# The ends of two mixers in a written order: rows stored as normed, scale and shift behind the gather, three blocks routed during the fourth, lists ahead of weights

## The chip, the cores and the metric

The kernel runs on one core of one Trainium2 chip. The metric is device time in microseconds of one execution, lower is better. A core has five engines with instruction queues of their own: TensorE (PE, matrix products and transposes), VectorE (DVE), ScalarE (ACT), GpSimd (POOL) and SyncE (SP), which here only issues transfers. ScalarE and GpSimd issue transfers too. Products are written to PSUM, everything else lies in SBUF, and inputs and weights come from HBM.

## What is computed

Two transformer blocks in a row on 512 tokens of width 1024, in float32. Each has a mixer and a mixture of experts. In the first, the experts are chosen in two levels (one of four groups, then two of its four experts); in the second, four of 32. Cut to what the change touches:

```python
# block 1, after the mixer
x = layer_norm(ALPHA * x + (1 + gt_m) * mix, ln1_g, ln1_b)
u = layer_norm(x) * (1 + sc_f) + sh_f        # no gain of its own: scale and shift by column
ffn = hierarchical_moe(u, ...)               # 16 experts, silu(u @ gate) * (u @ up) @ down
# block 2, after the mixer
x = x + gt1 * rmsnorm(y, g_post_mix)
h2 = rmsnorm(x, g_pre_ffn) * (1 + sc2) + sh2
f = moe_ffn(h2, w_router, b_router, w_gu, b_gu, w_dn, b_dn)   # 32 experts, top 4 of softmax
```

## The kernel before

Four stages follow one another: mixer1, moe1, mixer2, moe2. Tokens lie in four blocks (`c` = 0 to 3) of 128 rows. Matrix products are made in three passes on values split into a high part (`whi`, `xh`, written by ScalarE) and a low part (`wlo`, `xl`, written by VectorE as the difference).

**The end of a mixer.** mixer1 makes block `c` of its output with `tail_mm`, normalises it (`tail_norm`), stores it (X1), takes the statistics of the second norm, transposes the rows (`tail_turn`) for the router's logits, and `tail_u` writes the rows that the experts will read: ScalarE applies the norm, GpSimd multiplies by the row `1 + sc_f` and adds the row `sh_f` (L696, L697), and the result goes to HBM (U1). mixer2 does the same with `out_mm`, `tail_norm`, `tail_turn` and `tail_u`; there GpSimd multiplies by one row (L2188) and VectorE finishes (L2205) before the rows go to U2. The Tile scheduler orders all this by readiness and priority.

**Routing and lists.** When the logits of all four blocks are there, `route1` (or its twin at the end of mixer2) takes the top values, makes softmax weights, and `weights_of` makes a one-hot for each choice, the `mask` of chosen experts and their weights `comb`. `lists` turns the mask into each token's position in its expert's list by products with triangular ones (`pos`), and splits `comb` into three bfloat16 pieces (`w3`) in `aux`, beside the token's number. For an expert, `list_hot` marks which token stands at which place, `list_sum` multiplies that with `aux`, and `list_end` reads out the rows to gather (`ig`), to scatter (`isc`) and their weights (`slw`).

**The experts.** moe1 and moe2 run in an order written out by hand: steps (one for each weight slice), with hooks at step numbers. Up to 52 blocks of 128, 96, 64 or 32 rows are gathered from U by an indirect transfer on GpSimd's queue (`x_gather`), transposed on TensorE into PSUM (`x_turn`, tile `pt`), and split there into `xh` and `xl` (`x_split`); blocks of few rows stay whole and are copied (L1015). Weights come in 1 MB loads, most of them on SyncE's queue, into `wraw`, and are split by ScalarE and VectorE slice by slice. The first loads of a stage stand behind its first gather on GpSimd's queue. `plan` orders the experts' remainders into blocks once the counts are known; it runs on GpSimd (L854 on) in six pieces at the steps of the table PLAN, and gives SyncE the expert numbers (`exi`) for its further loads. mixer2's weight of the output and moe1's last loads share SyncE's queue with this.

## Time and profile before

| | us |
|---|---|
| median of three runs | 2361.54 |
| range of the runs | 2360.82 to 2361.91 |
| profiled execution | 2365.56 |
| its span | 2363.7 |

| stage | TensorE busy | VectorE busy | transfers busy |
|---|---|---|---|
| 420 to 700 us (moe1) | 247.48 of 280 | 179.50 of 280 | 0.94 |
| 1300 to 2364 us (moe2) | 955.53 of 1064 | 571.97 of 1064 | 0.98 |

A window row gives, for a stretch, the busy time of each engine in us, the granted clock of TensorE as a share of full, and the share of the sixteen transfer engines. A timeline row gives the start and the length of an instruction, what it writes and reads, and in brackets how long its engine stood idle before it and what ended that. Stages are limited by different things, so each row is read in its own stage.

### The profile page before, as it was taken

What the parts mean: (1) busy time and instruction counts of PE and PEld (TensorE: products, weight loads), DVE (VectorE), ACT (ScalarE), POOL (GpSimd) and SP (SyncE); (2) the same over time, 40 slices, a digit from 0 to 9 for tenths busy, and PEclk for the clock granted to TensorE, in tenths of its full rate; (3) what the DMA queues carried; (4) which work ended last, traced back from release to release, by engine and by line L of the source; (5) the groups of instructions that cost most, each with busy time, mean ns of one, the idle gap of its engine ahead of it and who ended that gap; (6) DMA issues with size and microseconds to landing.
All of it is one profiled execution on the core that took longest, in us unless ns stands there. A gap on an engine that the chain in (4) does not pass through costs nothing. (4 is left out here: it accounts for less than half of the span.)

```text
span 2363.7 us, 31489 instructions
## 1 busy us (share of the span) xinstructions
PE 2118.9 (90%) x11221; PEld 1357.3 (57%) x11221; DVE 1385.6 (59%) x2687; ACT 1024.0 (43%) x1560; POOL 432.8 (18%) x405
## 2 busy tenths in 40 slices
PE   6999996779997999999987989979999997999993
PEld 2656664446665887778865445635555563554551
DVE  5555597645786856664466456545455553654663
ACT  3332454435674544553234444424344433443553
POOL 2001223311312120000024211312211031112100
PEclk9999896989998999999997999989999998999996
DMA  9766446998986423313357999999999989999996
GB/s 291 241 205 237 177 172 257 353 355 309 356 292 205 103 76 111 109 58 118 130 181 282 383 405 399 363 375 403 403 395 395 405 342 379 403 401 398 398 409 229
DMA packets 174659, 679.80 MB, mean 288 GB/s; under 512 B 21293, under 2 KB 61061, under 8 KB 116129
## 3 DMA queue, kind: packets, MB, share of 16 engines
q1 hardware_dynamic: 151632, 606.83, 67.5%
q0 software_dynamic: 22576, 69.85, 10.6%
q8 instruction: 90, 1.47, 0.3%
q10 hardware_dynamic: 288, 1.05, 0.1%
q14 instruction: 73, 0.59, 0.1%
HBM read 642.29 MB, written 35.46 MB: 287 GB/s over the span
## 5 line engine op out<-in xcount | busy, mean ns | idle before, releaser
L121 DVE TENSOR_TENSOR wlo<-wraw,whi 128x1024 fp32r<-128x1024 f32 (+1 forms) x535 | 646.3, 1232 | 333.7 <-ACT whi L120 324.6
L120 ACT ACTIVATE whi<-wraw 128x1024 fp32r<-128x1024 f32 (+1 forms) x535 | 552.6, 1055 | 344.5 <-PE pm L83 124.7
L83 PE MATMUL pm<-whi,xh 128*96 128x512 f32 (+1 forms) x704 | 283.9, 404 | 15.1 <-ACT whi L120 15.0
L83 PE MATMUL pm<-wlo,xh 128*96 128x512 f32 (+1 forms) x704 | 281.0, 402 | 6.1 <-DVE wlo L121 5.5
L83 PE MATMUL pm<-wraw,xh 128*32 128x512 f32 (+1 forms) x1344 | 238.3, 617 | 12.6 <-DMA wraw<-in_w_gu 12.6
L83 PE MATMUL pm<-whi,xl 128*96 128x512 f32 (+1 forms) x608 | 243.0, 400 | 0.0
L996 POOL DMA_INDIRECT xg<-U,ig x52 | 88.5, 1701 | 631.2 <-issue 275.8
L1240 POOL DMA_INDIRECT Y<-eo,isc x52 | 99.2, 1908 | 402.8 <-ACT eo L1239 103.2
L83 PEld LDWEIGHTS pm<-whi,xh 128*96 128x96 f32 (+1 forms) x704 | 125.3, 178 | 64.3 <-ACT whi L120 20.4
L83 PEld LDWEIGHTS pm<-wraw,xh 128*32 128x32 f32 (+1 forms) x1344 | 68.1, 126 | 151.3 <-issue 124.0
L83 PEld LDWEIGHTS pm<-wlo,xh 128*96 128x96 f32 (+1 forms) x704 | 119.6, 170 | 50.3 <-DVE wlo L121 8.8
L83 PE MATMUL po<-wlo,ah 128*96 128x512 f32 (+1 forms) x304 | 124.2, 409 | 12.7 <-DVE wlo L121 12.4
L83 PE MATMUL po<-wraw,ah 128*32 128x512 f32 (+1 forms) x672 | 132.6, 620 | 1.9 <-DMA wraw<-in_w_dn 1.9
L83 PE MATMUL po<-whi,ah 128*96 128x512 f32 (+1 forms) x304 | 126.8, 417 | 8.1 <-ACT whi L120 6.3
L83 PEld LDWEIGHTS pm<-whi,xl 128*96 128x96 f32 (+1 forms) x608 | 106.4, 175 | 36.8
L83 PE MATMUL po<-whi,al 128*96 128x512 f32 (+1 forms) x304 | 121.8, 401 | 0.8 <-DVE al L1204 0.8
L1008 PEld LDWEIGHTS pt<-ident,xg 64*128 64x128 f32 (+3 forms) x416 | 56.5, 199 | 100.8 <-issue 51.8
L1008 PE MATMUL pt<-ident,xg 64*128 64x64 f32 (+3 forms) x416 | 70.0, 294 | 47.8 <-DMA xg<-U,ig 47.1
L1017 ACT ACTIVATE xh<-pt 128x384 fp32r<-128x384 f32 (+2 forms) x56 | 28.2, 504 | 130.1 <-PE pt L1008 114.8
L83 PE MATMUL px<-hh,whi 128*128 128x512 f32 x192 | 77.3, 403 | 0.6 <-DVE gsum L766 0.6
L83 PE MATMUL px<-hh,wlo 128*128 128x512 f32 x192 | 76.6, 399 | 0.0
L83 PE MATMUL px<-hl,whi 128*128 128x512 f32 x192 | 76.6, 399 | 0.0
(630 smaller groups left out, 3774.1 us busy)
## 6 DMA issues: line engine op xcount, KB each, us to landing
wraw<-in_w_gu SPq DMA_DIRECT2D x254, 1024.0 KB
wraw<-in_w_dn SPq DMA_DIRECT2D x126, 1024.0 KB
wraw<-in_w_e_down SPq DMA_DIRECT2D x31, 1024.0 KB
wraw<-in_w_e_gate SPq DMA_DIRECT2D x30, 1024.0 KB
wraw<-in_w_e_up SPq DMA_DIRECT2D x30, 1024.0 KB
wraw<-in_w_in SPq DMA_DIRECT2D x58, 512.0 KB
mz<-in_w_ada SPq DMA_DIRECT2D x80, 256.0 KB
wraw<-in_w_mod SPq DMA_DIRECT2D x26, 512.0 KB
```

The lines of the kernel that those rows point to most:

```text
L83: self.nc.tensor.matmul(out, lhsT, rhs, start=start, stop=stop)
L120: nc.scalar.activation(h, v, AF.Copy)
L121: nc.vector.tensor_sub(l, v, h.bitcast(F32))
L996: self.nc.gpsimd.indirect_dma_start(out=B.xg[0:B.n, :], out_offset=None, in_=self.U, in_offset=bass.IndirectOffsetOnAxis(ap=B.ig[:, :1], a ...
L1008: self.nc.tensor.transpose(B.xt[:, k * n:k * n + n], B.xg[0:n, 4 * h2 + k:1024:8], self.ident[0:n, 0:n])
L1017: nc.scalar.activation(B.xh[:, d, 0:n], pv, AF.Copy)
L1240: nc.gpsimd.indirect_dma_start(out=self.Y[:, :], out_offset=bass.IndirectOffsetOnAxis(ap=B.isc[:, :1], axis=0), in_=o, in_offset=None, com ...
```

## The change

It rewrites the end of both mixers and moves one step of arithmetic behind the gather.

- U1 and U2 hold the rows as normed: one pass of ScalarE with scale (and bias). GpSimd's row operations, VectorE's last pass in mixer2 and the broadcast rows are gone. The stores of blocks 2 and 3 are issued by ScalarE's queue in mixer1, by SyncE's in mixer2; the store of block 3's X1 goes to GpSimd's queue.
- `x_split` applies scale and shift to the transposed rows, where they are numbers per partition: four VectorE operations per half of a gathered block, in PSUM (or, for whole blocks, straight into the copy).
- The order from the last output product of mixer1, and from the second half of mixer2's products, is written by hand on TensorE, VectorE, ScalarE and GpSimd. Blocks 0 to 2 are routed up to the mask while block 3's root is worked out (`together` takes one operation of each in turn); block 3 follows alone.
- The mask is written as bfloat16. `lists` is divided: positions, the first experts' indices from three columns of `aux`, and only then softmax weights, `comb` and its three pieces.
- `rsqrt` loses one operation and writes to its target; in mixer2 two roots can run as one of width 2.
- `plan` runs on VectorE up to `exi`, at earlier steps. `ehalf` is made once at the start.
- Dummy products of the identity with itself (`warm`) are put into TensorE's order: 9 and 4 in mixer1, 8 and 4 in mixer2.

The core of the diff:

```diff
-PLAN = {2: (-4, -3, -1, 0, 1, 2), 1: (-4, -3, -1, 0, 1, 2)}
+PLAN = {2: (-11, -10, -9, -8, 1, 2), 1: (-11, -10, -9, -8, 1, 2)}
...
+    def together(self, *gs):
+        gs, r = list(gs), [None] * len(gs)
+        left = list(range(len(gs)))
+        while left:
+            for i in list(left):
+                try:
+                    next(gs[i])
...
         def tail_u(c):
-            cs = slice(c * 128, c * 128 + 128)
-            yc = y[:, c, :]
             u = wk.tile([128, 1024], F32, name="u", tag="L")
-            nc.scalar.activation(u, yc, AF.Identity, scale=sts[c][:, 1:2], bias=sts[c][:, 2:3])
-            nc.gpsimd.tensor_mul(u, u, rows[2])
-            nc.gpsimd.tensor_add(u, u, rows[3])
-            (nc.sync if c == 3 else nc.gpsimd).dma_start(self.U1[cs, :], u)
+            nc.scalar.activation(u, y[:, c, :], AF.Identity, scale=sts[c][:, 1:2], bias=sts[c][:, 2:3])
+            (nc.scalar if c > 1 else nc.gpsimd).dma_start(self.U1[c * 128:c * 128 + 128, :], u)
...
+            root = tail_stats(3)
+            l3 = tail_logits(3)
+            self.logit_end(R, 2, l2, sts[2][:, 1:2], sts[2][:, 0:1])
+            self.together(root, self.route1_steps(R.lg, Q, 0, 3))
+            self.logit_end(R, 3, l3, sts[3][:, 1:2], sts[3][:, 0:1])
+            tail_bias(3)
+            self.warm(9)
+            self.run_mod(self.route1_steps(R.lg, Q, 3, 1))
+            tail_u(3)
+            self.lists_pos()
+            self.warm(4)
+            ohs = self.lists_first(FIXED[1], lambda b: self.half_tile(wk.tile([128, 512], F32, name="loh", tag="P", bufs=7)))
+            self.route1_end(R.lg, Q, sm)
+            self.lists_comb(ohs)
...
+    def warm(self, n):
+        ps = self.pt.tile([128, 512], F32, name="pt")
+        for _ in range(n):
+            self.mm(ps[:, 0:128], self.ident, self.ident, True, True)
...
     def plan(self, fixed, pairs):
         nc, sm, L = self.nc, self.esm, self.L
-        ve, E = nc.gpsimd, L.E
+        ve, E = nc.vector, L.E
...
+        if self.xcols:
+            g, s = self.xcols
+            f = lo if B.col else pv
+            for k in range(4):
+                j = 4 * h2 + k
+                nc.vector.tensor_scalar(f[:, k, :], pv[:, k, :], g[:, j:j + 1], s[:, j:j + 1], op0=OP.mult, op1=OP.add)
+            pv = f
...
         def tail_u(c):
             q = xr[c // 2][:, c % 2, :]
-            nc.vector.scalar_tensor_tensor(q, q, rr[:, c:c + 1], rows[2], op0=OP.mult, op1=OP.add)
-            nc.gpsimd.dma_start(self.U2[c * 128:c * 128 + 128, :], q)
+            nc.scalar.activation(q, y[:, c, :], AF.Copy, scale=nr[:, c + 1, 1:2])
+            (nc.sync if c > 1 else nc.gpsimd).dma_start(self.U2[c * 128:c * 128 + 128, :], q)
...
+            for c in range(2):
+                out_end(c, 1, out_mm(c, 1, W))
+            tail_sum(0)
+            self.run_mod(root(0))
+            tail_norm(0)
+            out_end(2, 1, out_mm(2, 1, W))
+            tail_sum(1)
+            self.run_mod(root(1))
+            tail_norm(1)
+            tail_turn(0)
+            ps = out_mm(3, 1, W, None, range(4))
+            l0 = tail_logits(0)
+            tail_turn(1)
...
+            out_end(3, 1, out_mm(3, 1, W, ps, range(4, 8)))
```

VectorE at the end of mixer1, from the mask to the first indices, before (`ohk` one-hot of the choices, `ew` weights, `slsb` the sum read out):

```order
L807 TENSOR_REDUCE mask<-ohk 128x64
L1528 RECIPROCAL s_3359<-s_3359 128x4
L817 CAST maskb<-mask 128x64
L1529 TENSOR_TENSOR ew<-s_3359,gw 128x4
L1530 TENSOR_TENSOR ew<-ew,e_3358 128x4
L808 TENSOR_TENSOR ohk<-ohk,ew 128x128
L827 SCALAR_TENSOR_TENSOR pos<-px,mask 128x64
L809 TENSOR_REDUCE comb<-ohk 128x64
L829 TENSOR_SCALAR pos<-pos 128x64
L840 COPY cnt<-px 128x16
L921 CAST aux<-comb 128x64
L929 TENSOR_TENSOR oh<-slots,pos 128x512
```

and with the change:

```order
L896 TENSOR_REDUCE maskb<-ohk 128x16
L933 SCALAR_TENSOR_TENSOR pos<-px,maskb 128x64
L935 TENSOR_SCALAR pos<-pos 128x64
L1049 TENSOR_TENSOR loh<-slots,pos 128x512 x2
L1067 COPY slsb_3398<-pt 128x3
L972 TENSOR_SCALAR plank<-cnt 128x16
L1071 TENSOR_TENSOR slf_3402<-slsb_3398 128x1
L973 TENSOR_TENSOR plank<-plank,slots 128x16
L1072 CAST ig_3400<-slf_3402 128x1
```

The weights and their split are no longer between positions and indices, and the first pieces of the plan (`plank`) stand there instead.

VectorE at the start of moe1, from the end of the lists to the first block's split, before:

```order
L954 TENSOR_REDUCE slw<-slsb 128x1
L858 TENSOR_REDUCE planc<-plano 16x1
L1019 TENSOR_TENSOR xl<-pt,xh 128x512
L861 TENSOR_REDUCE planc<-plano 16x1
L1019 TENSOR_TENSOR xl<-pt,xh 128x512
L121 TENSOR_TENSOR wlo<-wraw,whi 128x1024 x4
```

and with the change:

```order
L1042 CAST aux<-w3r_3432 128x64
L1043 TENSOR_TENSOR aux<-w3r_3432,aux 128x64
L957 TENSOR_REDUCE slw_3442<-pt 128x1
L957 TENSOR_REDUCE slw_3449<-pt 128x1
L996 CAST exi<-plan 1x16
L1152 TENSOR_SCALAR pt<-pt,g_1894,s_1896 128x128 x4
L1159 TENSOR_TENSOR xl<-pt,xh 128x512
L1152 TENSOR_SCALAR pt<-pt,g_1894,s_1896 128x128 x4
L1159 TENSOR_TENSOR xl<-pt,xh 128x512
L121 TENSOR_TENSOR wlo<-wraw,whi 128x1024 x4
```

Weights' pieces, their sums and `exi` now stand here, and the four operations of scale and shift ahead of each half's low part.

ScalarE at the end of mixer2 (`q` squares: of a product `px` with `ss`, of normed rows `y`; `uT` and `rows` transposes copied out, `l` logits), before:

```order
L2178 ACTIVATE q_11526,ss_4299<-px 128x512
L2192 ACTIVATE q_11548,ss_4299<-y_11301 128x1024
L2178 ACTIVATE q_11591,ss_4299<-px 128x512
L2192 ACTIVATE q_11613,ss_4299<-y_11301 128x1024
L2178 ACTIVATE q_11656,ss_4299<-px 128x512
L2192 ACTIVATE q_11678,ss_4299<-y_11301 128x1024
L2199 ACTIVATE uT<-pt 128x512 x2
L778 ACTIVATE l_11755<-px 128x128
L2199 ACTIVATE rows_11302<-pt 128x512 x2
```

and with the change:

```order
L2341 ACTIVATE q_11673,ss_4351<-px 128x512
L2362 ACTIVATE q_11693,nv<-y_11431 128x1024
L2341 ACTIVATE q_11720,ss_4351<-px 128x512
L2362 ACTIVATE q_11743,nv<-y_11431 128x1024
L2370 ACTIVATE uT<-pt 128x512 x2
L858 ACTIVATE l_11780<-pw 128x128
L2370 ACTIVATE rows_11432<-pt 128x512 x2
L2362 ACTIVATE q_11815,nv<-y_11431 128x1024
L2383 ACTIVATE xr_11434<-y_11431,nr 128x1024
L2341 ACTIVATE q_11832,ss_4351<-px 128x512
L858 ACTIVATE l_11844<-pw 128x128
L2370 ACTIVATE uT<-pt 128x512 x2
```

The copies of block 0's and 1's transposes now stand ahead of the square of block 3's product, behind the squares of the normed rows of blocks 0 and 1.

## Rows read from the trace of the kernel before

**Rows 1.** Windows by stage: PE, PEld, DVE, ACT, POOL busy; clock; DMA share; GB/s
```profile
370.00:380.00 10.00, 0.90 (x22) 0.82 (x22) 6.31 (x36) 0.20 (x1) 3.15 (x5) 0.50 0.26 89
1240.00:1250.00 10.00, 0.81 (x18) 0.72 (x18) 9.64 (x31) 0.00 (x0) 3.31 (x4) 0.50 0.01 2
420.00:700.00 280.00, 247.48 (x1229) 160.11 (x1229) 179.50 (x305) 157.08 (x227) 61.91 (x45) 0.93 0.94 342
1300.00:2364.00 1064.00, 955.53 (x4682) 528.85 (x4674) 571.97 (x801) 443.36 (x553) 193.72 (x139) 0.95 0.98 382
```

**Rows 2.** Timeline of GpSimd, end of mixer1: start, length, instruction, idle before
```profile
353.55 2.86 POOL L697 TENSOR_TENSOR u<-u,rows 128x1024 f32<-128x1024 f32 x1
...
376.55 1.05 POOL L996 DMA_INDIRECT xg<-U,ig  x1 [7.80 <-DVE slf L949]
```

**Rows 3.** Timeline of GpSimd, end of mixer2
```profile
1247.75 1.60 POOL L996 DMA_INDIRECT xg<-U,ig  x1 [0.18 <-issue]
```

**Rows 4.** Timeline of VectorE, end of mixer1
```profile
354.70 1.73 DVE L155 SCALAR_TENSOR_TENSOR rs<-rs,rs 128x1 f32<-128x1 f32 x1
...
357.78 1.28 DVE L674 SCALAR_TENSOR_TENSOR ymix<-ymix,rs,rows 128x1024 f32<-128x1024 f32 x1
...
371.38 0.20 DVE L817 CAST maskb<-mask 128x64 bf16<-128x64 f32 x1
...
375.54 0.15 DVE L950 CAST ig<-slf 128x1 int32<-128x1 f32 x1
```

**Rows 5.** Timeline of VectorE, end of mixer2
```profile
1229.98 3.44 DVE L2205 SCALAR_TENSOR_TENSOR xr<-xr,rr,rows 128x1024 f32<-128x1024 f32 x1
...
1238.03 0.25 DVE L785 SCALAR_TENSOR_TENSOR lg<-px,rr,br 128x32 f32<-128x32 f32 x1 [0.26 <-PE px L83]
...
1246.56 0.15 DVE L950 CAST ig<-slf 128x1 int32<-128x1 f32 x1
...
1247.08 3.60 DVE L121 TENSOR_TENSOR wlo<-wraw,whi 128x1024 fp32r<-128x1024 f32 x3
```

**Rows 6.** Timeline of TensorE, start of moe1
```profile
380.99 1.94 PE L1008 MATMUL pt<-ident,xg 128*128 128x128 f32 x8 [5.78 <-DMA xg<-U,ig]
...
388.46 0.78 PE L83 MATMUL pm<-whi,xh 128*128 128x512 f32 x1
```

**Rows 7.** Timeline of TensorE, end of mixer2 and start of moe2
```profile
1231.36 0.54 PE L83 MATMUL px<-ssum,l 128*128 128x32 f32 x2 [1.95 <-ACT l L778]
...
1260.07 0.63 PE L83 MATMUL pm<-whi,xh 128*128 128x512 f32 x1
1260.50 0.63 PE L83 MATMUL pm<-wlo,xh 128*128 128x512 f32 x1
```

**Rows 8.** Groups by line, shapes apart: busy, mean ns, idle before and releaser
```profile
L155 DVE SCALAR_TENSOR_TENSOR rs<-rs,rs 128x1 f32<-128x1 f32 x90 | 21.6, 256 | 1.0
...
L588 DVE SCALAR_TENSOR_TENSOR ol<-px,chn,oh 128x128 fp32r<-128x128 f32 x16 | 5.5, 343 | 0.5 <-ACT oh L587 0.4 <-PE pm L83 0.2
```

**Rows 9.** Transfers issued from 350 to 381 us: count, size, us to landing
```profile
U<-u POOLq DMA_DIRECT2D x1, 512.0 KB, 2.9
```

**Rows 10.** Transfers issued from 1216 to 1245 us
```profile
U<-xr POOLq DMA_DIRECT2D x4, 512.0 KB, 4.1
```

**Rows 11.** Timeline of ScalarE, end of mixer2
```profile
1211.38 0.60 ACT L2178 ACTIVATE q<-px 128x512 f32<-128x512 f32 x1 [4.91 <-PE px L83]
...
1216.88 0.60 ACT L2178 ACTIVATE q<-px 128x512 f32<-128x512 f32 x1 [3.78 <-PE px L83]
...
1223.31 1.06 ACT L2192 ACTIVATE q<-y 128x1024 f32<-128x1024 f32 x1
```

**Rows 12.** Windows (columns as rows 1), end of mixer2 and first experts of moe2
```profile
1230.00:1234.00 4.00, 2.64 (x22) 1.46 (x23) 4.00 (x10) 3.39 (x7) 3.17 (x3) 0.69 0.26 104
1280.00:1290.00 10.00, 8.80 (x43) 6.99 (x42) 9.79 (x22) 7.48 (x10) 7.84 (x3) 1.00 0.72 275
```

**Rows 13.** Waits of the queue of SyncE from 400 us on: total, times, longest
```profile
SPq L107 <- DVE wlo L121: 524.7, 157, 23.9
```

More of the change, by code (lines that the diff above doesn't have):

```diff
@@ L204, in consts @@
         nc.vector.memset(self.half[0:64, 1:2], 1.0)
+        self.ehalf = cp.tile([128, 2], F32, name="ehalf")
+        for s in range(2):
+            nc.vector.memset(self.ehalf[64 - 64 * s:128 - 64 * s, s:s + 1], -1.0)
+            for a in (2 * s, 2 * s + 1):
+                ps = slice(32 * a, 32 * a + 32)
+                nc.vector.tensor_scalar(self.ehalf[ps, s:s + 1], self.pcol[ps, :], -32.0 * a, None, op0=OP.add)
         self.zero1 = cp.tile([128, 1], F32, name="zero1")
@@ L708, in mixer1 @@
         self.mload = self.raw_halves
-        for n in range(16 + 14):
+        for n in range(19):
             if n >= 8:
@@ L721, in mixer1 @@
                 att_sum(units[n - 3])
-            for c in (3, 2, 1, 0):
+            for c in (2, 1, 0):
                 d = n - (4 * c + 3)
@@ L777, in logits @@
         l4 = self.tiny.tile([128, 128], F32, name="l4", bufs=2)
-        nc.scalar.activation(l4, ps[:, 0:128], AF.Copy)
-        p2 = self.px.tile([128, 512], F32, name="px")
+        self.nc.scalar.activation(l4, ps[:, 0:128], AF.Copy)
         self.mm(p2[:, 0:32], l4, R.ssum, True, True)
-        d = p2[:, 0:32]
+        return p2[:, 0:32]
+    def logits(self, R, c, xT, r, m=None):
+        nc = self.nc
+        self.logit_end(R, c, self.logits_mm(R, xT, *[self.px.tile([128, 512], F32, name="px") for _ in range(2)]), r, m)
@@ new lines, in mask_steps @@
+    def mask_steps(self, E, K, xf, oh, c0, n):
+        nc, cs = self.nc, slice(c0, c0 + n)
+        nc.vector.tensor_tensor(oh[:, cs], self.slots[:, None, None, 0:E].to_broadcast([128, n, K, E]),
+                                xf[:, cs, 0:K, None].to_broadcast([128, n, K, E]), op=OP.is_equal)
+        yield
+        with nc.allow_low_precision(reason="sums of zeros and a one"):
+            nc.vector.reduce_sum(self.L.mask[:, cs, :], oh[:, cs].rearrange("p c k e -> p c e k"), axis=AX)
+        yield
@@ new lines, in route1_tiles, with route1_steps @@
+    def route1_tiles(self, sm):
+        Q = type("Q", (), {})()
+        Q.g, Q.e = self.top_tiles(sm, "g"), self.top_tiles(sm, "e")
+        Q.d = sm.tile([128, 4, 4], F32, name="gd")
+        Q.sel = sm.tile([128, 4, 16], F32, name="sel")
+        Q.oh = sm.tile([128, 4, 2, 16], F32, name="ohk")
+        return Q
+    def route1_steps(self, lg, Q, c0, n):
+        nc, cs = self.nc, slice(c0, c0 + n)
+        self.top8(lg[:, :, 0:8], None, "g", c0, n, Q.g)
+        yield
+        nc.vector.tensor_tensor(Q.d[:, cs], self.slots[:, None, 0:4].to_broadcast([128, n, 4]),
+                                Q.g[2][:, cs, 0:1].to_broadcast([128, n, 4]), op=OP.is_equal)
+        yield
+        nc.vector.tensor_scalar(Q.d[:, cs], Q.d[:, cs], -NEG, NEG, op0=OP.mult, op1=OP.add)
+        yield
+        for c in range(c0, c0 + n):
+            nc.vector.tensor_tensor(Q.sel[:, c, :].rearrange("p (g e) -> p g e", g=4),
+                                    lg[:, c, 16:32].rearrange("p (g e) -> p g e", g=4),
+                                    Q.d[:, c, :, None].to_broadcast([128, 4, 4]), op=OP.add)
+        yield
+        self.top8(Q.sel, None, "e", c0, n, Q.e)
+        yield
+        yield from self.mask_steps(16, 2, Q.e[2], Q.oh, c0, n)
@@ L2154, in mixer2 @@
         rt = bg.tile([128, 4, 1024], F32, name="rows2", tag="B")
-        rows = [rt[:, i, :] for i in range(3)]
-        self.bcast_row(rows[0], self.dap(RW, 0, [[1, 1024]]))
-        self.bcast_row(rows[1], self.dap(RW, 1024, [[1, 1024]]))
-        self.bcast_row(rows[2], self.dap(self.mod2, 3 * 1024, [[1, 1024]]))
+        row = rt[:, 0, :]
+        self.bcast_row(row, self.dap(RW, 0, [[1, 1024]]))
         xr = [bg.tile([128, 2, 1024], F32, name=f"xr{a}", tag="JE"[a]) for a in range(2)]
@@ L2239, in moe2 @@
         bias = self.V.bias
-        esel = self.esm.tile([128, 1], F32, name="esel")
-        nc.vector.tensor_copy(esel, self.pcol)
-        for a in range(1, 4):
-            ps = slice(32 * a, 32 * a + 32)
-            nc.vector.tensor_scalar(esel[ps, :], esel[ps, :], -32.0 * a, None, op0=OP.add)
         def src_of(e):
```

382 lines of the change are left out of this document (233 added, 149 removed).

## The prediction

> **What bounds the kernel now.** I read the windows by stage first. From 420 to 700 us and from 1300 us to the end the transfers are busy for 0.94 and 0.98 of the time, TensorE for 0.88 and 0.90, VectorE for 0.64 and 0.54 [rows 1]: the two expert stages run at the pace of the weight stream. The two ends of the mixers do not. In 370 to 380 us and 1240 to 1250 us TensorE works 0.8 to 0.9 us of ten, the transfers have a share of 0.26 and 0.01, and VectorE is at 6.31 and 9.64 [rows 1]. So a weight stream that starts earlier ends earlier, and what starts it stands on GpSimd's queue behind the gather of the first rows: 376.55 us in the first end, 1247.75 us in the second [rows 2, 3]. The timelines of VectorE show what the gather waits for: a chain of small operations up to the row indices `ig` (375.54 and 1246.56 us) [rows 4, 5]. From the gather to the first expert matmul it is another 11.9 us (388.46) and 12.3 us (1260.07) [rows 6, 7].
>
> **The first end.** (a) GpSimd's multiply and add with the shift and scale rows go. Beside one such add (353.55 us, 2.86 us long) a Newton step of VectorE on 128x1 took 1.73 us, against a mean of 0.26 us [rows 2, 4, 8]. Without that, and with the second normalisation pass (357.78 us) following its root after eight steps at a pitch of 0.2 us, I put the end of block 3's rows at 356.3 us, 2.7 us earlier than 359.06. (b) From there to the mask cast (371.38 us) it took 12.3 us [rows 4]. Now block 2's logits and the three first blocks' routing fill VectorE while block 3's statistics, transposes and logits run: 28 operations at about 0.2 us, from 358.3 to 364.2. Block 3's logits are ready by 361, so VectorE sets the pace; then eleven operations for block 3 alone, mask at 367.2: 10.9 us, 1.4 us less. (c) Mask to indices took 4.2 us [rows 4], behind the softmax weights' split; now position, two one-hots and the sum: 3.6 us, `ig` at 370.8. The other condition for the gather is block 3's stored rows: ScalarE can write them at 366.1, its own queue issues the store, and stores of this size landed after 2.9 and 4.1 us on GpSimd's queue [rows 9, 10], so 369 to 370.2 and not last. Gather at 371.3, **5.2 us earlier**. (d) Behind the gather the plan of the later blocks is hidden now, but scale and shift come in: four operations of 128x128 from PSUM per half, two halves. The nearest row is 0.34 us [rows 8]; the dependent four of a half make 1.4 us. They stand behind the weights, the split and the plan on VectorE (31 operations of about 0.2 us, free at 377.6 us, when the transposes of the first half, after a gather that lands 4.4 us after its issue as now [rows 2, 6], are also done). Two halves with their high and low parts end at 382.7 on ScalarE; the first weight's high part then takes 1.05 us and its low part 1.25 us more, so the matmuls run from about 384.2. That is 12.9 us from the gather instead of 11.9: **1.0 us given back**. First end: 4.2 us gained, with 3 to 6 as bounds.
>
> **The second end.** (e) GpSimd's row multiply goes here too: beside it VectorE's pass over 128x1024 took 3.44 us [rows 5], where 1.28 us is the rule [rows 4]; that pass moves to ScalarE altogether. (f) But the new written order puts something on the path that sets the end. ScalarE works in order, and there the square of block 1's normed rows now stands ahead of the two copies of block 0's transposes, and TensorE's order has block 0's logits and block 1's transposes in the middle of the last output block. The squares of an output block start 5.5 us apart [rows 11], so block 2's is at 1216.9. VectorE starts block 0's root only after block 1's product (1212.8), block 1's root and normed rows end at 1222.05, the square takes 1.06 us [rows 11] and about 1.2 with its sum read out, the copies follow from 1223.3. TensorE has done block 0's transposes and half of block 3's product by 1220.9 and waits about 3 us. The last product ends at 1229.2 instead of 1222.3. From there: product 0.8, sum and two-wide root 2.3, norm 1.2, square 1.2 (ahead of the copies again), and the last mask pieces and root interleaved on VectorE: block 3's logits at 1239.3, against 1238.03 [rows 5]. (g) Behind them the gain comes: `ig` took 8.5 us from that row before (with a reduction of 128x512, the weights' split and the bias columns on the way) [rows 5], now one block's top-8, a reduction of 128x32, positions, one one-hot and the sum: 3.9 us, 1243.2. The stored rows need the last root (1239.2), ScalarE's pass of 1.15 us and 2.9 to 4.1 us [rows 9, 10]: 1243.3 to 1244.5. Gather at 1244.2, **3.5 us earlier**, if TensorE keeps its clock. (h) After it VectorE has the weights, the split, the plan and three low halves (3.60 us, which stood right behind the indices before [rows 5]) ahead of scale and shift, about 10 us, and TensorE's plan products stand ahead of the transposes of the gathered rows: first matmul 12.6 us after the gather, 0.3 us more than now.
>
> TensorE's clock decides (g). Before, the granted clock was 0.69 of full in 1230 to 1234 us and 0.50 through 1240 to 1250, after idle spells of about 2 us between thin products [rows 1, 7, 12]. If the new 3 us spell brings it to 1.2 GHz, half a product (12 matmuls) costs 0.43 instead of 0.23 us each [rows 7], 2.4 us, and the transposes behind it 1 us: the gather would be at 1247.5 and the end gains nothing. I take a value between the two ends, a gain of 2.2 us, with 0 and 4 as bounds.
>
> The Trainium skill, "TensorE: Matmul & The Clock Gate", section on the HAM clock gate, says that the throttled rate is the default and only sustained activity lifts it. By that the dummy products that the change adds (13 in the first end, 12 in the second) are too thin to hold the clock, and the lower end, no gain in the second end, would be right. The windows of before agree that thin work does not hold it.
>
> **The expert stages.** 432 scale-and-shift operations over 52 blocks are added to VectorE. At 0.24 to 0.34 us (128x32 to 128x128) they are some 125 us of 1340, while ScalarE loses 48 copies. VectorE goes from 0.54 to 0.61 in the second stage. Where the transfers are the bound I cost them at nothing: the weight stream hides them. The bounds are 0 and 8 us, from the places where VectorE is full already (9.79 of 10 in 1280 to 1290 us [rows 12]). The plan on VectorE and the earlier `exi` let SyncE go on sooner, but the loads of 1 MB each that stand behind the gather on GpSimd's queue cover that time, so nothing. The loads that the scheduler moved on SyncE (the second half of a mixer weight, a counter) wait for work that is done about when they are reached: nothing, 2 us as upper bound.
>
> A rule that speaks against the change stands in the Trainium skill, "SBUF — State Buffer", section on practical consequences: descriptors of a transfer issued by GpSimd cannot be written while VectorE holds the shared port pair. The rows: the gather's issue took 1.05 us with VectorE idle and 1.60 us with it in low halves [rows 2, 3]. Now VectorE works beside all three gathers; by the rule up to 0.55 us each would be lost, about 1.5 us of the sum.
>
> **Sum.** 4.2 + 2.2 = 6.4 us. The profiled execution took 2365.56 us, its span 2363.7; the median of the runs is 2361.54, and I take the difference from that: **2355.1 us**.
>
> **Rivals.** (R1) Slower: VectorE becomes the pace-setter of the weight stream. SyncE's loads waited 525 us, 157 times, for a low half of VectorE to free its buffer [rows 13], so VectorE is in the loop that issues loads. Against it: transfers at 0.98 with VectorE at 0.54. If each of the 30 split blocks delays the low halves by its eight operations, 2.5 us, and 6 of them show because nothing is queued then, it costs 15 us: 2370. It decides from three such blocks on. (R2) The ends give nothing: in the second the half clock, in the first the stores land last (twice the 2.9 us of rows 9 would put the gather at 372), and moe1's slack swallows the rest: 2360. (R3) The ends give the whole length that the order promises: TensorE stays warm, blocks 0 to 2 are truly hidden, the ramp of the second stage (transfers 0.72 in 1280 to 1290 us) starts with three low halves done: 6 + 7 = 13 us, 2349.
>
> **Chances.** Forecast (2352 to 2358.5) 0.42, R3 (under 2352) 0.18, R2 (2358.5 to 2364) 0.24, R1 (over 2364) 0.16. What a measurement can tell from no change is about 0.2%, 4.7 us. Below 2356.8: R3 and most of the forecast, 0.52. Within 2356.8 to 2366.3: 0.34. Above: 0.14. The range leaves out a tenth on each side: 2347 to 2367.
>
> **What would show it.** First end: gather near 371.3, first expert matmul near 384, no VectorE step over 0.4 us on 128x1 from 350 to 372. Second end: a TensorE wait of about 3 us near 1221 (less the first end's gain), the last output product about 7 us later against its start than before, block 3's logits no earlier, gather 0 to 4 us earlier. Experts: transfers at 0.98 still, VectorE 0.61. Wrong, if the last product of the second end is not delayed (gain up to 10 us there), or if the transfer share of the expert stages falls.

## The result: slower by 1.8 percent, and the profile after

The changed kernel takes 2403.48 us (median of six runs, 2399.62 to 2412.68), the kernel before beside it 2361.72 us: 1.0176 times the time, 95% interval 1.0152 to 1.0199. The forecast was 2355.1 us with a range up to 2367. The profiled execution took 2407.2 us, its span 2405.4.

The span is cut at the same landmarks in both traces: the two first gathers on GpSimd, the first expert product and the last one of a stage on TensorE, the square of mixer2's third output block (second half) on ScalarE. Each number is the difference of two start times, or of a start and an end.

| part of the span, us | before | after | difference |
|---|---|---|---|
| start to first gather | 376.55 | 369.07 | -7.5 |
| to the first expert product | 11.91 | 16.31 | +4.4 |
| expert stage 1 | 321.09 | 348.27 | +27.2 |
| mixer2 to the square | 507.33 | 514.63 | +7.3 |
| square to second gather | 30.87 | 28.28 | -2.6 |
| to the first expert product | 12.32 | 13.52 | +1.2 |
| expert stage 2 and the end | 1103.63 | 1115.32 | +11.7 |

So the ends gained 3.1 and 1.4 us, near the 4.2 and 1.9 of the forecast, and the expert stages, costed at nothing, lost 38.9. The table is one execution of each kernel: in the nine kernels of this document with the first end of the change the first gather came at 367.88 to 374.17 us, in the six with the old one at 375.50 to 378.37. So the first row is a gain of 6.1 us in the mean, and a single one can be 3 us off. The landmarks of after, from the timelines of GpSimd and TensorE (start, length, instruction, idle before and what ended it), answer to [rows 2, 3, 6, 7]:

```profile
369.07 1.07 POOL L1124 DMA_INDIRECT xg<-U,ig  x1 [11.65 <-DVE ig L1072]
...
385.38 0.80 PE L83 MATMUL pm<-whi,xh 128*128 128x512 f32 x1 [2.15 <-ACT whi L120]
...
1276.56 1.06 POOL L1124 DMA_INDIRECT xg<-U,ig  x1 [6.78 <-DVE rs L2440]
...
1290.08 0.79 PE L83 MATMUL pm<-whi,xh 128*128 128x512 f32 x1 [1.27 <-ACT xh L1158]
```

Windows of after (busy us of PE, PEld, DVE, ACT, POOL; clock; share of the transfers; GB/s), against [rows 1]. In 420 to 700 us TensorE falls from 247.48 to 233.14 us and VectorE rises from 179.50 to 198.11. The share of the transfers falls from 0.94 to 0.93 (342 to 332 GB/s), which the prediction had named as a sign of being wrong, if by little. The second row lies behind the whole length of the old stage: VectorE is at ten of ten, the transfers at 0.16.

```profile
420.00:700.00 280.00, 233.14 (x1132) 145.92 (x1131) 198.11 (x405) 134.66 (x193) 65.12 (x44) 0.92 0.93 332
...
710.00:720.00 10.00, 10.00 (x47) 7.04 (x46) 10.00 (x11) 9.13 (x12) 5.73 (x1) 1.00 0.16 19
```

The groups by line (busy us, mean ns of one, idle of the engine before them and what ended it), two of after and then one of before, show the added operations in the split blocks and who waits for them: ScalarE's high parts `xh` sit behind VectorE's scale and shift for 220.8 us. The same copies of before sat 130.1 us, most of it for TensorE.

```profile
L1158 ACT ACTIVATE xh<-pt 128x384 fp32r<-128x384 f32 (+2 forms) x56 | 28.5, 510 | 223.4 <-DVE pt L1152 220.8 <-DMA wraw<-in_w_dn 2.6
L1152 DVE TENSOR_SCALAR pt<-pt,rwa,rwc 128x96 f32<-128x96 f32 (+2 forms) x128 | 49.7, 389 | 52.4 <-PE pt L1136 48.9
```

```profile
L1017 ACT ACTIVATE xh<-pt 128x384 fp32r<-128x384 f32 (+2 forms) x56 | 28.2, 504 | 130.1 <-PE pt L1008 114.8 <-POOL plano L860 15.0
```

And this is what windows of ten microseconds would have shown in the trace of before. Of the 32 from 390 to 710 us, eleven have VectorE at 8.5 of ten or more, four of them at 9.8 or more, and in nine of the eleven the transfers are at 0.96 or more as well; others go down to 1.5. The mean of [rows 1], 0.64, hides both. Of the three shown, the first and the last have seven and eight low halves of weights in them, which go with split blocks, the middle one has one:

```profile
410.00:420.00 10.00, 9.22 (x44) 6.67 (x43) 9.83 (x19) 6.37 (x8) 3.72 (x5) 1.00 0.98 338
540.00:550.00 10.00, 10.00 (x49) 7.50 (x48) 3.76 (x17) 2.12 (x4) 0.00 (x0) 1.00 0.59 214
...
660.00:670.00 10.00, 10.00 (x47) 7.80 (x46) 9.97 (x10) 8.53 (x11) 0.00 (x0) 1.00 1.03 399
```

### The profile page after: what moved, and what is told of

Same layout as the page of the kernel before. It is cut to its first block, busy times and chain, and to the rows that moved or that the text cites. A ratio compares the mean times of both kernels' runs of the same rounds, so it can differ in the third digit from the quotient of the medians.

```text
span 2405.4 us, 31908 instructions
## 1 busy us (share of the span) xinstructions
PE 2137.8 (89%) x11283; PEld 1368.7 (57%) x11283; DVE 1504.3 (63%) x3055; ACT 1011.5 (42%) x1518; POOL 403.3 (17%) x368
## 5 line engine op out<-in xcount | busy, mean ns | idle before, releaser
L83 PE MATMUL pm<-wlo,xh 128*96 128x512 f32 (+1 forms) x704 | 280.6, 401 | 11.7 <-DVE wlo L121 11.6
L83 PE MATMUL po<-wlo,ah 128*96 128x512 f32 (+1 forms) x304 | 128.1, 422 | 12.3 <-DVE wlo L121 11.8
L1158 ACT ACTIVATE xh<-pt 128x384 fp32r<-128x384 f32 (+2 forms) x56 | 28.5, 510 | 223.4 <-DVE pt L1152 220.8
L1152 DVE TENSOR_SCALAR pt<-pt,rwa,rwc 128x96 f32<-128x96 f32 (+2 forms) x128 | 49.7, 389 | 52.4 <-PE pt L1136 48.9
L83 PEld LDWEIGHTS po<-wlo,ah 128*96 128x96 f32 (+1 forms) x304 | 55.5, 182 | 40.0 <-DVE wlo L121 23.3
```

Of the source, the lines that this page charges most:

```text
L83: self.nc.tensor.matmul(out, lhsT, rhs, start=start, stop=stop)
L1152: nc.vector.tensor_scalar(f[:, k, :], pv[:, k, :], g[:, j:j + 1], s[:, j:j + 1], op0=OP.mult, op1=OP.add)
L1158: nc.scalar.activation(B.xh[:, d, 0:n], pv, AF.Copy)
```

## The experiments

Theory S: VectorE's scale and shift cost the expert stages their time. Rivals: P, the plan on VectorE; Q, the loads that the scheduler moved on SyncE. Later S was divided: B, VectorE paces the loop, and what is added to it is paid; C, ScalarE is blocked, in order, behind VectorE's operations.

**e1_no_scale.** The changed kernel without scale and shift; whole blocks are copied by ScalarE.

```diff
-        if self.xcols:
+        if False:
```

> The changed kernel with the scale and shift behind the gather left out (whole blocks are copied by ScalarE again); the experts get the rows without scale and shift, so this leaves out a part of the computation. Theory S (the scale-and-shift operations on VectorE pace the expert stages): moe1 from its first matmul to its last goes from 348 back to about 321 us and moe2 from 1115 to about 1104, the kernel to about 2363 us (0.983 of the changed kernel, about the kernel before). Theory P (the plan on VectorE and at earlier steps delays the weight stream): moe1 stays near 345, the kernel near 2400. Theory Q (loads that moved on SyncE's queue hold up weights): also near 2400.

2354.6 us, 0.9954 times before (0.9938 to 0.9971), 8 us under what S expected. Stage 1 takes 324.3 us, stage 2 1092.8: against after the operations cost 24.0 + 22.5 = 46.5 us in the profiled executions (48.9 between the medians of the whole time). S holds; everything else in the change is a small gain. This kernel leaves scale and shift out; e8_rows_scaled below, which has them ahead of the store, has the same two stage times within 1.1 us.

**e2_before_scale.** The same operations added to the kernel before.

```diff
+        f = B.xf[:, d, 0:n] if B.col else pv
+        for k in range(4):
+            nc.vector.tensor_scalar(f[:, k, :], pv[:, k, :], self.one1, self.zero1, op0=OP.mult, op1=OP.add)
```

> The kernel before with only the 432 VectorE operations put in at the same place (times one, plus zero, in place of ScalarE's copies for whole blocks). Theory S: 2361.5 + 35 to 40 = about 2398 us, and ScalarE's high parts wait for these operations (some 80 us in moe1 alone). Theories P and Q: 2362 to 2367 us, since plan and loads are as before.

2418.92 us, 1.0228 (1.0211 to 1.0245); stage 1 346.9 us, stage 2 1120.8. The loss comes without the rest of the change. It is larger than the expected 2398 us: the profiled spans are 53 us apart, of which 42.9 lie in the two stages and 6.5 between the gathers and the first expert products.

**e3_scalar_scale.** The changed kernel with scale and shift on ScalarE.

```diff
-  nc.vector.tensor_scalar(f[:, k, :], pv[:, k, :], g[:, j:j + 1], s[:, j:j + 1], op0=OP.mult, op1=OP.add)
+  nc.scalar.activation(f[:, k, :], pv[:, k, :], AF.Identity, scale=g[:, j:j + 1], bias=s[:, j:j + 1])
```

> The changed kernel with scale and shift made by ScalarE (four activations with scale and bias) instead of VectorE, in the same place. If only the busy time matters (theory S as load): ScalarE at 0.42 has room, VectorE falls from 0.63 to 0.58, about 2365 us. If the coupling of the two engines' orders is what costs (high part waits for VectorE, whose low parts wait for ScalarE's high parts): also recovered, since one engine makes scale and high part, 2363 to 2368 us. If any work of about 0.3 us each in this chain costs what it lasts: no better than 2395 us. Theories P, Q: near 2400.

2372.26 us, 1.0029 (1.0017 to 1.0041); stage 1 330.8, stage 2 1095.9. The same number of operations costs 9.6 us over e1_no_scale in the stages of the profiled executions instead of 46.5, and 17.7 between the medians instead of 48.9 (the profiled execution was one of the fastest). The time is more than S expected (about 2365 us) and far from the 2395 of the third theory: about two thirds of the loss go with the engine. The Trainium skill, "Perfetto Trace Analysis", section on optimizing Scalar/DVE operations, says that offloading to ScalarE may make sense when VectorE is saturated; this run agrees.

**e4_old_plan.** The changed kernel with the plan on GpSimd at its old steps.

```diff
-        ve, E = nc.vector, L.E
+        ve, E = nc.gpsimd, L.E
...
-PLAN = {2: (-11, -10, -9, -8, 1, 2), 1: (-11, -10, -9, -8, 1, 2)}
+PLAN = {2: (-4, -3, -1, 0, 1, 2), 1: (-4, -3, -1, 0, 1, 2)}
```

> The changed kernel with the plan back on GpSimd and at the steps of before. Theory P: moe1 back to about 325 us, the kernel to about 2370. Theory S: moe1 stays near 348; first matmul of each expert stage 2 to 3 us later than in the changed kernel; 2403 to 2410 us.

2409.28 us, 1.0193 (1.0176 to 1.021): as the changed kernel. P falls. Q falls with e2_before_scale, as the cause of the stages' loss, for that kernel has it with the old order of loads.

**e5_before_load.** The kernel before, the operations writing to a spare tile.

```diff
+        u = self.esm.tile([128, 128], F32, name="dum", bufs=1)[:, 0:n]
+        for k in range(4):
+            nc.vector.tensor_scalar(u, pv[:, k, :], self.one1, self.zero1, op0=OP.mult, op1=OP.add)
```

> The kernel before with the same 416 VectorE operations on the same PSUM tiles and at the same places, but with their results in a spare tile of SBUF that nothing reads: ScalarE's high part waits for TensorE's transposes, as before, and no longer for VectorE. Theory B (busy time: VectorE's low halves of the weights come later by what stands ahead of them in its order): the loss of e2_before_scale comes back, 2405 to 2420 us, expert stage 1 near 345 us. Theory C (coupling: ScalarE, which works in order, sits behind VectorE's scale operations with its next high parts): near the kernel before, 2361 to 2372 us, stage 1 at 321 to 327 us.

2417.44 us, 1.0229 (1.0211 to 1.0246). Taken alone this would speak for B, but the run did not separate the two: the waits of the trace in 425 to 600 us (total, times, longest) show ScalarE still waiting for VectorE, because the build orders the two readers of one PSUM tile.

```profile
ACT xh L1020 <- DVE dum L1016: 37.6, 11, 6.9
ACT xh L1018 <- DVE dum L1016: 36.8, 10, 7.4
```

**e9_before_sbuf.** So the spare operations read and write SBUF.

```diff
+        u = self.esm.tile([128, 128], F32, name="dum", bufs=1)
+        for k in range(6):
+            nc.vector.tensor_scalar(u, self.ident, self.one1, self.zero1, op0=OP.mult, op1=OP.add)
```

> The kernel before with six VectorE operations of 128x128 from SBUF to a spare tile of SBUF ahead of each half's high part (624 operations at some 0.23 us, 144 us; the 416 scale operations are 150 us). They wait for nothing and nothing waits for them; ScalarE's high part waits for TensorE's transposes as before. In e5_before_load the build still made ScalarE wait for the spare operations, because they read the same PSUM tile; that is gone here. Theory B (VectorE's busy time ahead of its low halves): 2405 to 2420 us, stage 1 near 345 us. Theory C (ScalarE, in order, stands behind VectorE): 2362 to 2373 us, stage 1 at 321 to 328 us.

2398.27 us, 1.0151 (1.0134 to 1.0167); stage 1 338.8, stage 2 1113.5. This is outside both ranges, 7 us under B's and 25 over C's: work on VectorE whose results nothing reads costs 35 us. It took more than the 144 us of the expectation, since one lasted 0.375 us (six in 2.25): VectorE's busy time rises from 1385.6 to 1589.1 us.

**e10_defer_high and e12_defer_more.** The changed kernel, high and low parts half a step behind scale and shift; in e12 all of it later, with the second end of e11_defer_j2.

```diff
+    def x_part(self, B):                                 # the end of x_split, now by itself
...
                     at(i + 0.5, self.x_split, B, h2)     # e12: i + 1
+                    at(i + 1, self.x_part, B)            # e12: i + 2; high and low part
```

> The changed kernel, its high and low parts of the rows recorded one half step later than scale and shift, so that in the written order ScalarE has the high part of the next weight half between its wait and VectorE's scale operations; every operation is kept. Theory C: most of the time of the expert stages comes back, stage 1 at 325 to 335 us instead of 348, 2360 to 2380 us in all. Theory B: VectorE's work is the same, so 2395 to 2405 us.

> e11_defer_j2 with scale and shift a half step and the high and low parts another half step later (transposes at a step, scale one step behind them, parts two steps). Theory C in its wider form, that any wait of the in-order ScalarE or VectorE in this place costs the weight stream (before, ScalarE waited 115 us there for TensorE's transposes): 3 to 15 us under e11_defer_j2. If that wait was free: the same within 2 us, or later where the rows come too late for their products.

2403.23 us, 1.0162 (1.0142 to 1.0181), and 2411.83 us, 1.0212 (1.0195 to 1.0229); stage 1 350.7 and 357.8. In e10_defer_high the wait of ScalarE's high parts for VectorE fell from 220.8 to 136.3 us, and the time did not follow. Stage 2 alone is 6.8 us shorter than in after (1108.5 against 1115.3), stage 1 2.5 longer. C falls as the main cause; that it has a few microseconds in it isn't excluded.

**e6_cols_only.** Scale and shift only in the whole blocks.

```diff
-        if self.xcols:
+        if self.xcols and B.col:
```

> The changed kernel with scale and shift only in the 24 small blocks that stay whole (192 operations); the 28 blocks that are split into high and low parts (224 operations) keep their rows as normed, so this kernel leaves out a part of the computation. In the small blocks ScalarE has nothing to do behind VectorE's operations. Theory C (ScalarE waits for VectorE in the split blocks): 2355 to 2363 us, within 0.3% of e1_no_scale. Theory B (the time goes with the number of VectorE operations): 2354.6 + 49 x 192/416 = 2377 us.

2427.92 us, 1.0267 (1.0247 to 1.0287), outside both expectations. Stage 1 gives the answer, 326.3 us against 324.3 without any and 348.3 with all of them: the 96 operations in split blocks cost 22 us, the 48 in whole blocks 2. The second stage can't be used: other rows out of stage 1 change the second router's choice, and the trace has 559 high parts of weights instead of the 535 of all other kernels here.

**e13_spare_split and e14_spare_whole** ask the same with unchanged routes: e9_before_sbuf's spare operations in one kind of block alone.

```diff
-        for k in range(6):
+        for k in range(0 if B.col else 6):     # e14: 6 if B.col else 0
```

> e9_before_sbuf with its six spare operations of VectorE per half only in the 28 split blocks (336 operations at 0.375 us, 126 us). If VectorE's work costs time where the low halves fill it: the whole loss of e9_before_sbuf, 2392 to 2400 us. If it costs by busy time wherever it stands: 2363 + 35 x 336/624 = 2382 us.

> The same with the spare operations only in the 24 blocks that stay whole (288 operations, 108 us), where no low halves are made and VectorE is at 2.4 to 5.2 of ten: 2361 to 2367 us if the place decides, 2363 + 35 x 288/624 = 2379 us if busy time alone does.

2391.29 us, 1.0119 (1.0102 to 1.0136), and 2368.6 us, 1.0029 (1.0018 to 1.0039), beside 2361.53 us of before. 126 us of spare work (six operations in 2.25 us) cost 30 in split blocks, 108 us cost 7 in whole ones. Each is just outside the range that I gave for "the place decides" (2392 to 2400 and 2361 to 2367 us) and 9 to 10 us from the number for busy time alone. Stage 1 says the same: 338.8 us in e13_spare_split, as in e9_before_sbuf, and 327.0 in e14_spare_whole, against 321.1. Place decides more than busy time, though whole blocks are not free, which I had expected them to be; and even in split blocks a quarter of the work's length is paid, not all of it.

**e7_turn0_first.** One line of the second end moved.

```diff
             out_end(2, 1, out_mm(2, 1, W))
+            tail_turn(0)
...
             tail_norm(1)
-            tail_turn(0)
```

> The changed kernel with one line moved in the second end: the transposes of block 0 and their copies stand right behind the third output block, ahead of block 1's root, norm and square. Theory of step (f): ScalarE's copies no longer stand behind block 1's square, the wait of TensorE for uT (3.3 us) is gone, the last output product ends 3 us earlier, and the second gather starts 2.5 to 3.5 us earlier against the square of the third output block (25 to 26 us behind it instead of 28.3): 2400 us. Rival: the chain through the roots of VectorE sets the end, and the gather is less than 1 us earlier: 2403 us.

2404.32 us, 1.0165 (1.0148 to 1.0182). The last output product ends 10.6 us behind the third block's square instead of 13.8, and the last mask 22.8 instead of 24.6, so the line did what step (f) says. But the gather stands 28.26 us behind that square instead of 28.28. The window 1265 to 1270 us and the timelines of TensorE and VectorE, of e7_turn0_first and then of after, show why:

```profile
1265.00:1270.00 5.00, 3.93 (x27) 2.60 (x27) 4.72 (x22) 3.80 (x8) 2.19 (x4) 0.50 1.00 390
...
1270.33 3.76 PE L83 MATMUL pt<-ident 128*128 128x128 f32 x16
...
1274.40 0.29 DVE L933 SCALAR_TENSOR_TENSOR pos<-px,maskb 128x128 f32<-128x128 f32 x1 [2.04 <-PE px L83]
```

```profile
1265.00:1270.00 5.00, 2.95 (x41) 1.74 (x34) 4.70 (x21) 3.71 (x8) 2.41 (x4) 1.00 0.87 313
...
1270.43 2.03 PE L83 MATMUL pt<-ident 128*128 128x128 f32 x16
...
1273.56 0.29 DVE L933 SCALAR_TENSOR_TENSOR pos<-px,maskb 128x128 f32<-128x128 f32 x1 [0.19 <-PE px L83]
```

The granted clock is at its lower level (0.50), the eight dummy products (two passes each, 16 rows) take 3.76 instead of 2.03 us, and the mask's products stand behind them.

**e11_defer_j2.** e10_defer_high with block 0's logits ahead of block 1's norm as well, and two dummy products instead of eight.

```diff
             out_end(2, 1, out_mm(2, 1, W))
+            tail_turn(0)
+            ps = out_mm(3, 1, W, None, range(4))
+            l0 = tail_logits(0)
...
-            self.warm(8)
+            self.warm(2)
```

> e10_defer_high with the second end rewritten: block 0's transposes, their copies and its logits stand ahead of block 1's root, norm and square, and 2 dummy products instead of 8 stand ahead of the last block's mask products (in e7_turn0_first, at a granted clock of 0.50, the 8 took 3.76 us and VectorE waited 2.04 us for the products behind them). If both stood on the path to the gather: the second gather 3 to 5 us earlier than in e7_turn0_first (23.5 to 25.5 us behind the square of the third output block instead of 28.3), and the time 3 to 5 us under e10_defer_high. If VectorE's chain sets the end: the same time as e10_defer_high within 2 us.

2402.67 us, 1.0166 (1.0147 to 1.0185). The gather stands 27.5 us behind the square against 30.9 in e10_defer_high, but only 0.8 us better than after, whose 28.28 the expectation was set against; the 23.5 to 25.5 us that I expected are missed. With the same second end e12_defer_more has 26.9. The time is that of e10_defer_high within 2 us. That VectorE's chain sets the rest of this end is what is left, not shown by itself.

**e8_rows_scaled.** The order of the change, with rows scaled before the store as before.

```diff
+                nc.gpsimd.tensor_mul(u, u, rows[2])     # blocks 0 to 2; block 3: two VectorE passes
+                nc.gpsimd.tensor_add(u, u, rows[3])
...
-        if self.xcols:
+        if False:
```

> The changed kernel with the line of e7_turn0_first moved, and with the rows scaled and shifted before they are stored, as in the kernel before (blocks 0 to 2 of the first end and 0 to 2 of the second partly on GpSimd, the last one on VectorE), so that nothing stands between transposes and high parts. If the expert stages lost their time to the scale operations alone: 2352 to 2358 us, faster than the kernel before by 0.2 to 0.4%. If the row operations beside VectorE's routing take back what the new order gives: 2358 to 2364 us, no difference from before.

2362.47 us, 0.9991 (0.9981 to 1.0001). The stages are back, 323.3 and 1093.0 us; the ends are not: first gather at 380.12, second 33.4 us behind the square. The timelines of GpSimd and VectorE of this run show [rows 2, 4] again, one long step beside the multiply and one beside the add:

```profile
357.74 3.10 POOL L750 TENSOR_TENSOR u<-u,rows 128x1024 f32<-128x1024 f32 x1 [6.60 <-ACT u L749]
360.92 2.00 POOL L751 TENSOR_TENSOR u<-u,rows 128x1024 f32<-128x1024 f32 x1
...
358.74 2.11 DVE L158 SCALAR_TENSOR_TENSOR rs<-rs,rs 128x1 f32<-128x1 f32 x1
361.08 1.85 DVE L158 SCALAR_TENSOR_TENSOR rs<-rs,rs 128x1 f32<-128x1 f32 x1
```

**e15_rows_early and e16_rows_dve.** e8_rows_scaled with block 2's rows elsewhere, mixer2's column product on GpSimd and the second end of e11_defer_j2.

```diff
-            nc.vector.tensor_mul(a, a, b)
+            nc.gpsimd.tensor_mul(a, a, b)
...
+            tail_u(2)                 # e15: ahead of block 2's transposes
             tail_turn(2)
...
             tail_norm(3, stats)
+            tail_u(2)                 # e16: here, two passes of VectorE
```

> e8_rows_scaled with three changes: the product of the scale columns in mixer 2 on GpSimd instead of VectorE; in the first end block 2's rows go to GpSimd before its transposes instead of behind its logits (there, beside the multiply, two Newton steps of 128x1 took 2.11 and 1.85 us); in the second end block 0's logits ahead of block 1's norm and 2 dummy products instead of 8. If these are the three places: mixer 2 at 507 to 509 us instead of 511.5, the first gather at 374 to 377 us instead of 380, the second gather 30 to 32 us behind the square of the third output block instead of 33.4; 2352 to 2357 us, faster than before by 0.3 to 0.4%. Otherwise 2360 to 2364 us, as e8_rows_scaled.

> e15_rows_early with block 2's rows of the first end scaled by VectorE (two passes of 1.28 us behind block 3's norm) and GpSimd free. If the multiply on GpSimd is what slows the Newton steps wherever it stands: first gather at 375 to 377 us, at or ahead of e15_rows_early. If its earlier place already cured that: 1 to 3 us behind it.

2361.9 us, 0.9999 (0.9984 to 1.0013), and 2362.15 us, 1.0003 (0.9993 to 1.0014). The first gather comes to 373.78 and 374.84. Both lie in the range of e15_rows_early, but 1.1 us between two kernels is less than this gather wandered in kernels with one order, so the question of e16_rows_dve stays open. The second gather stays at 33.9 us behind the square, and mixer2 takes 514.4 and 510.6 us, so the column product was not its loss. No kernel that computes the whole thing beat the kernel before.

## Why the prediction was wrong, point by point

**The step that failed** is "where the transfers are the bound I cost them at nothing: the weight stream hides them", with bounds of 0 and 8 us. It cost 46.5 us (after against e1_no_scale). The price of the operations themselves was near: some 125 us forecast, and VectorE is busy for 1504.3 us instead of the 1369.8 of e1_no_scale, 134.5 more. What failed is the overlap. I read one mean over a stage in which two kinds of block alternate, and took the one full window that I had ([rows 12], 9.79 of ten) for an exception worth 8 us. In split blocks VectorE makes the low halves of the weights, and at the fullest it is at 9.8 to 10 of ten while the transfers are at 0.98 to 1.03 (the windows above). What is added to VectorE there is paid in part: 30 of 126 us in e13_spare_split, 46.5 of those 134.5 us here. VectorE's share was forecast well (0.62 in 1300 to 2364 us, forecast 0.61), and the transfers were at 0.98 in that window before and after, which shows how little both shares say.

**R1** named the mechanism, with the right unit (eight operations per split block) and the wrong count. It let 6 of 30 blocks show, 15 us, at a chance of 0.16. There are 28, and 46.5 us over 28 is 1.7 us for each, of the 3.1 that eight operations of 0.385 us last. The count of operations is 416, not 432. The wait that R1 rested on, that of SyncE's loads for a low half of VectorE from 400 us on [rows 13], answers it: 524.7 us before, and in after, e1_no_scale and e3_scalar_scale

```profile
SPq L107 <- DVE wlo L121: 663.4, 177, 23.9
```

```profile
SPq L107 <- DVE wlo L121: 527.0, 154, 23.9
```

```profile
SPq L107 <- DVE wlo L121: 590.8, 175, 24.0
```

A second way from VectorE to the end stands beside it, and no run tells the two apart. Transposed rows and transposed activations share two PSUM buffers (`pt`), and TensorE's transposes of the activations stand in order behind the rows' low parts `xl`, which free a buffer. In stage 2 that wait was 5.6 us in before, and in after and e1_no_scale

```profile
PE pt L1285 <- DVE xl L1159: 23.4, 10, 3.6
```

```profile
PE pt L1285 <- DVE xl L1159: 5.6, 5, 1.2
```

It was 20.3 us in e9_before_sbuf. So it is shown that VectorE's added work in split blocks costs the time; whether by the weights' low halves or by the rows' low parts coming late is not. A kernel with another number of `pt` buffers would have been the experiment.

Why scale operations cost more than spare ones: in stage 1, VectorE's busy time grew by 44.6 us in e2_before_scale for 25.8 us of stage, by 66.8 us in e9_before_sbuf for 17.7 (of these 66.8, about a third stands in whole blocks). The waits of VectorE in that stage, of before, e9_before_sbuf and e2_before_scale, suggest an answer:

```profile
DVE xl L1019 <- ACT xh L1017: 15.4, 5, 7.1
DVE xh L1019 <- ACT xh L1017: 10.8, 4, 6.9
```

```profile
DVE xh L1022 <- ACT xh L1020: 2.9, 1, 2.9
```

```profile
DVE pt L1016 <- PE pt L1008: 13.4, 5, 5.4
DVE xl L1021 <- ACT xh L1019: 10.9, 18, 0.7
```

Spare work fills the wait for the transposed rows (26.2 us before, 2.9 of it left among the longest waits); scale and shift stand behind that wait and add a second one. This is argued from the waits, not tested by itself.

**First end.** (a) held: no step on 128x1 lasts over 0.4 us there, and e8_rows_scaled brings the long ones back with the multiply and the add. The gather came at 369.07, 2.2 us before the 371.3 of (b) and (c). (d) was mis-sized: 16.3 us from gather to product instead of 12.9. So the near hit of this end, 3.1 us gained of 4.2, is two errors against each other, and luck in that.

What (d) left out is TensorE's order. The gather landed 4.3 us after its start, as I had it, but the plan's products, now at earlier steps, stand ahead of the transposes (timeline of TensorE):

```profile
375.52 2.31 PE L83 MATMUL pt<-planm,plant 16*128 16x16 f32 x10 [0.68 <-ACT plant L987]
377.76 1.97 PE L1136 MATMUL pt<-ident,xg 128*128 128x128 f32 x8
```

So scale and shift start 9.9 us behind the gather instead of the 6.3 of (d). From there the two halves take 5.5 us up to the second high part where I had 5.1: a half's four operations last 1.78 us where I had 1.4 (timeline of VectorE):

```profile
378.93 1.78 DVE L1152 TENSOR_SCALAR pt<-pt,g,s 128x128 f32<-128x128 f32 x4 [0.62 <-PE pt L1136]
381.37 0.69 DVE L1159 TENSOR_TENSOR xl<-pt,xh 128x512 fp32r<-128x512 f32 x1 [0.66 <-ACT xh L1158]
381.98 1.77 DVE L1152 TENSOR_SCALAR pt<-pt,g,s 128x128 f32<-128x128 f32 x4
```

**Second end.** (f) held in its place and size: block 1's square (1253.33 us) stands ahead of the copies on ScalarE, TensorE waits 3.3 us, forecast about 3, and the last output product ends 13.8 us behind the third block's square, forecast 12.3 (before: 5.6):

```profile
1253.33 1.06 ACT L2362 ACTIVATE q<-y 128x1024 f32<-128x1024 f32 x1 [4.38 <-DVE nv L2353]
...
1254.39 1.06 ACT L2370 ACTIVATE uT<-pt 128x512 f32<-128x512 f32 x2
...
1255.11 0.82 PE L83 MATMUL pw<-uT,wr 128*32 128x128 f32 x16 [3.32 <-ACT uT L2370]
```

(g) gave 2.6 us against the forecast of 2.2, (h) took 1.2 against 0.3. That the clock decides (g) held. e10_defer_high has the same second end as after, but its clock was 0.50 there and its gather came 30.89 us behind the square, no earlier than the 30.87 of before (window and timeline of TensorE of e10_defer_high):

```profile
1275.00:1280.00 5.00, 4.38 (x31) 3.48 (x32) 4.00 (x17) 3.89 (x5) 0.85 (x2) 0.50 0.69 279
...
1277.29 3.57 PE L83 MATMUL pt<-ident 128*128 128x128 f32 x16
```

So the 2.2 us between the two ends were a fair bet, and which end a kernel gets differs between kernels with one order. By the Trainium skill, "TensorE: Matmul & The Clock Gate", section on the HAM clock gate, as I read it, the thin products would not hold the clock and nothing would be gained. In after it was 1.00 in 1265 to 1270 us, with TensorE busy 4.27 of five in the five before; in e7_turn0_first, with 2.71 of five there, it was 0.50, and the 1.9 us by which its last mask stood earlier were gone at the gather. So the measurement sides with that reading of the Trainium skill in e7_turn0_first and e10_defer_high and against it in after.

**The other rule** of the Trainium skill, "SBUF — State Buffer", section on practical consequences, that VectorE on the shared ports keeps GpSimd from writing descriptors, would have cost up to 0.55 us per gather. I had misread one of its two rows: beside the issue of 1.05 us [rows 2] VectorE was not idle but at small operations up to 377.03 us. The gathers of after were issued in 1.07 and 1.06 us with VectorE at small operations beside them: nothing was lost here. In e1_no_scale, e3_scalar_scale and e4_old_plan the second one took 1.37 to 1.41 us.

**Not in the sum:** mixer2's 7.3 us, which every kernel of the new order lost in some measure (3 to 7 us; e2_before_scale 1.3, e9_before_sbuf 0.9), and a second stage that is 10.8 us shorter than before once the operations are out (1092.8 in e1_no_scale, 1093.0 in e8_rows_scaled, 1103.6 before). Both stay open. The plan's engine is not the cause of the first (e4_old_plan: 511.6 us), nor is the column product; the loads that moved on SyncE, which the prediction priced at up to 2 us, were tested by no run there. About half of the second lies at the start of the stage: in the 70 us from 30 us before the first expert product on, the transfers moved 263 GB/s in before, 293 in e1_no_scale, 295 in e8_rows_scaled and 294 in after, some 2 MB more, which is some 5 us at the 382 GB/s of the stage. That is the ramp of R3; in after the 22.5 us of the operations hide it.

## What to carry to other kernels

A stage's mean busy share says nothing on where an added operation lands. Cut the stage into windows as long as one unit of its work and look for those in which the engine that is to get the operation is full; count these, and charge each for a part of what is added (here a quarter to a third of its length). Work that stands behind a wait seems to cost more than work that can fill it, as far as the waits above tell. And when arithmetic is moved off a short serial end into a long loop, weigh one saving against the number of passes: 4.5 us of ends stood here against 28 blocks.

## What the runs showed that I had not expected

- Dummy products meant to hold the clock are a cost when it falls: at 0.50 of full, eight took 3.76 instead of 2.03 us, in order ahead of the products that were waited for.
- ScalarE's operation with a scale and a bias per partition took 0.40 us, mostly on 128x96, VectorE's with two scalars 0.39 (medians 0.403 and 0.385 us over blocks of 64 to 128 rows): moved one for one, the loss fell from 48.9 to 17.7 us between medians. ScalarE was at 6.4 to 8.5 of ten in the two windows above where VectorE was at 9.8 to 10.
- A multiply and an add of 128x1024 on GpSimd stretched VectorE steps of 128x1 to 2.11 and 1.85 us (0.22 without them), but not the pass over 128x1024 that had begun 0.37 us before the multiply (1.27 us). The 3.44 us of [rows 5] are such a pass that began within 0.01 us of a multiply.
- Two engines that only read the same PSUM tile were put in order by the build, so a spare reader is not free of coupling (37.6 us of waits in e5_before_load).
